# S5 products on VectorE alone, O in whole rows, layer 1's attention bias beside layer 0's merge

## The chip, the cores and the metric

One core of a Trainium2 chip runs the kernel, in float32, as one program. The metric is the device time of one execution in microseconds; several executions are taken and their median is given. TensorE's clock has two levels, 1.2 and 2.4 GHz; the profile shows what was granted, as a share of full speed.

## What is computed

A backbone of two layers over 512 latent tokens and 256 context tokens, 1024 channels. Each layer projects the normalised, modulated input by one wide matrix and hands the parts to three mixers: a bidirectional S5 state-space model, a neighbourhood attention with a learned bias by relative position, and a latent attention with compressed keys. Cut to what the change touches:

```python
h = layer_norm(x) * (1.0 + scale) + shift
(ua, za, qn, kn, vn, zn, cq, ckv, kr, zm, ga, gn, gm) = split_cols(h @ w_in)
# S5, for each direction d and each of 32 groups, state of 64 complex numbers:
s[t] = a * s[t - 1] + (bb @ u[t]);  y[t] = real(c @ s[t])
# neighbourhood attention: bias[h] = rpb[h, row offset, column offset], masked outside the window
s_lat = (q @ k.T) * NA_SCALE + bias
m = sig(ga) * ((ya * silu(za)) @ w_branch_a) + sig(gn) * ((yn * silu(zn)) @ w_branch_b) \
  + sig(gm) * ((ym * silu(zm)) @ w_branch_c)
x = layer_norm(DEEPNORM_ALPHA * x + gate * (m @ w_out))
```

The S5 recurrence is computed in chunks of 8 tokens. For that, small matrices are built from the parameters alone: W (inputs of a chunk to its state), O (state to outputs), the rotations R and the kernel K inside a chunk, out of powers of `a` and of B and C.

## The kernel before

A layer runs in five stages, each in a block `with phase(...)`: `s5a` (projections for S5, the gates and the compressed keys, and the S5 matrices), `na` (S5 itself and neighbourhood attention), `mla`, `mrg` (the merge, with gates and branch products) and `out`. A planner inside the compiler puts each engine's instructions and DMA issues in order from a timeline that it estimates; it draws on the order in the program. Every engine works off its list in that order, and so does SyncE's DMA queue, called `Q`, on which all DMAs of the parts that follow are issued.

Every matrix product is done in three float32r parts. A weight is loaded into one of four buffers `wr` (`wraw`, line 212), copied by ScalarE to `wh`, and the rest `wl` is a subtraction on VectorE or GpSimd (`split`, line 204), two buffers each; `gemm` (line 226) then runs the matmuls of line 233. The compressed keys have matmuls of their own at line 1054, with loads at line 1046.

`s5_build` (line 560) makes the S5 matrices of one block of 8 groups; there are four blocks a layer. `prm` holds tables of powers that `s5_tables` made. For each direction 12 elementwise products and sums run on `sb` tiles, a ring of six (`SB`, four in the merge): six for R (lines 630 to 636), three for O (649 to 651), three for W (677 to 679). Each string of `BE` says, letter by letter, which engine makes which of these 12: P is GpSimd, V is VectorE. `BE[0]` serves layer 0's four builds in its stage `s5a`, `BE[2]` layer 1's builds in layer 1's stage, `BE[1]` the builds of layer 1 that run early, in layer 0's merge, in halves of four groups. Results go to DRAM: R at line 637, O at 653, W at 684, K at 685, and from K the Toeplitz matrix by line 688. Line 661 holds the small matmuls on O that make K; line 679's result is transposed on TensorE. `s5_block` (line 692) loads these matrices in stage `na`, O at line 710, and multiplies with them.

`na_bias` (line 341) makes the attention bias of both layers: it writes the reversed, padded table to DRAM (`rpb_d`, line 348), then, for each layer and each pair of heads, three loads with overlapping rows fill a tile of the `sb` ring (line 359), GpSimd adds the mask `na_mk`, and line 361 stores it to `na_zd`. It is called once, in layer 0's stage `s5a`, by the letter N of `JOBS[0]`, the job order `uuBaBmaBmBacmaNmc`; B is a build, a and m are gate projections, c a half of the compressed keys, u an S5 input.

In layer 0's merge `SIDE[0]` says which side work goes before which of 24 steps: T makes layer 1's tables, B a build (`next_build`, line 1457), G gelu (line 1460) of S5's output, which closes the pools of T and B and takes memory behind them. Steps 0 to 7 are branch b, 8 to 15 branch c with its gates, from 16 on the remaining gates of branch a; then come the GLU products on gelu's result `ah`.

Of the kernel before, what the change touches and what calls it, by code (L numbers as in the profile page):

```python
# [78 lines left out]
BE = ('PPVVPVVPVVPV', 'VVPVVVVVVVVV', 'VPVVPVVPVVPV')  # L79
# [6 lines left out]
SIDE = ('T....B.B......G.........', '................G.......')  # L86
# [34 lines left out]
def build(tc, a, out):  # L121
# [219 lines left out]
    def na_bias(p, wk):  # L341
# [9 lines left out]
        zs = []  # L351
        for l in range(DEPTH):
            zd = T(dr, [48, 8, 480], f"na_zd{l}")
            for h2 in range(4):
                z = T(wk, [128, 1152], "sb", SB[0])[0:48, 0:960].rearrange("p (r c) -> p r c", c=32)
                for ty in range(3):
                    src = bass.AP(tensor=pd.tensor, offset=pd.offset + (l * 8 + 2 * h2) * 960 + 8 * ty,
                                  ap=[[1, 16], [64, 30], [1, 32]])
                    Q.dma_start(out=z[16 * ty:16 * ty + 16], in_=src)
                tt(P, z, z, mk.unsqueeze(1).to_broadcast([48, 30, 32]), ALU.add)  # L360
                Q.dma_start(out=zd[:, 2 * h2:2 * h2 + 2], in_=z.rearrange("p (h r) c -> p h (r c)", h=2))
            zs.append(zd)
        return zs
# [196 lines left out]
    def s5_build(l, b, prm, wk, ng, be, nsb, ni):  # L560
# [15 lines left out]
        od = [T(dr, [128, 1024], f"s5_o{l}{b}{d}") for d in range(2)]  # L576
# [38 lines left out]
        E = [V if c == 'V' else P for c in be]  # L615
        np_ = ng // 2
        for d in range(2):
            w = T(wk, [128, 1024], "s5_w", 1)
            for h in range(8 // ng):
# [10 lines left out]
                tt(E[0], rv[0], A[0], B[0], ALU.mult)  # L630
                tt(E[1], r1.rearrange("p c (x y) -> p c x y", x=6), A[1], B[1], ALU.mult)
                tt(E[2], rc[:, 0], rc[:, 0], r1, ALU.subtract)
                tt(E[3], rv[1], A[0], B[1], ALU.mult)
                r2 = sb(np_, 96)
                tt(E[4], r2.rearrange("p c (x y) -> p c x y", x=6), A[1], B[0], ALU.mult)
                tt(E[5], rc[:, 1], rc[:, 1], r2, ALU.add)
                Q.dma_start(out=rd[d][:, :, 96 * np_ * h:96 * np_ * (h + 1)], in_=rc.rearrange("p z c n -> p z (c n)"))
# [11 lines left out]
                tt(E[6], o, cc[0], pw[0], ALU.mult)  # L649
                tt(E[7], t, cc[1], pw[1], ALU.mult)  # L650
                tt(E[8], o, o, t, ALU.add)
# [25 lines left out]
                tt(E[9], x, bc[0], pw[0], ALU.mult)  # L677
                tt(E[10], t, bc[1], pw[1], ALU.mult)
                tt(E[11], x, x, t, ALU.add)
# [4 lines left out]
            Q.dma_start(out=wd[d], in_=w)  # L684
        Q.dma_start(out=kd.rearrange("x q n -> q x n"), in_=kds.rearrange("p x m i -> p x (m i)"))
# [6 lines left out]
    def s5_block(mats, b, m8, ud, yd, p, need_ctx):  # L692
# [10 lines left out]
        for d in range(2):  # L703
# [54 lines left out]
        for g in range(8):  # L758
            o = py[:, 512 * (g // 4) + 96 * (g % 4):][:, 0:NY]
            PE.matmul(o, tp[:, g], u[:, g, 32:32 + NY], start=True, stop=False)  # L760
            PE.matmul(o, ot[0][:, g], sd[0][:, g, 32:32 + NY], start=False, stop=False)
            PE.matmul(o, ot[1][:, g], sd[1][:, g, 1:1 + NY], start=False, stop=True)
# [903 lines left out]
```

## Time and profile before

| What | Value |
|---|---|
| Time, median of 3 runs | 1876.83 us (1871.46 to 1877.72) |
| The profiled execution | 1875.92 us, of which the span of the trace is 1874.1 us |
| TensorE matmul, busy | 1699.5 us, 91% |
| VectorE, busy | 1274.9 us, 68% |
| ScalarE, busy | 746.8 us, 40% |
| GpSimd, busy | 733.9 us, 39% |
| Mean granted clock of TensorE | 0.960 |
| DMA | 262.90 MB, mean 140 GB/s |

The table is an average over the whole span; what a change in one stage can be worth is read from that stage. In the rows, PE is TensorE, DVE VectorE, ACT ScalarE, POOL GpSimd and SP (SPq) SyncE with its DMA queue; L661 is line 661. A group's line names operation, output tile and input tiles, shapes and count.

### The profile page before, as it was taken

How to read it: one execution, taken by the hardware profiler on the slowest of the kernel's cores; microseconds unless marked ns; L12 is line 12 of the kernel's file. 1: busy time of each engine (PE TensorE's matmuls, PEld its weight loads, DVE VectorE, ACT ScalarE, POOL GpSimd, SP SyncE). 2: the span in 40 equal slices, each digit the busy share in tenths (PEclk: the TensorE clock that was granted, in tenths of full speed). 3: DMA queues.
4: the chain of work that ended last, by engine and by line, in shares of the span. 5: the costliest groups of instructions: out<-in, count | busy, mean ns of one | idle time of the engine just before them, and what ended most of it. 6: DMA issues, size and time to landing. Idle time of an engine off the chain costs nothing. (4 is left out here: it accounts for less than half of the span.)

```text
span 1874.1 us, 29013 instructions
## 1 busy us (share of the span) xinstructions
PE 1699.5 (91%) x10808; PEld 1406.4 (75%) x10808; DVE 1274.9 (68%) x2531; ACT 746.8 (40%) x1466; POOL 733.9 (39%) x472
## 2 busy tenths in 40 slices
PE   4877689999999999898999988799999999999987
PEld 2666578888878887777787766687888878788865
DVE  4999935687766556699735597944888866653267
ACT  4422233443365556222233335342444455652241
POOL 2177753223422111323445857723333221135373
PEclk9888899999999999999999999899999899999998
DMA  9546595443431120655637725565454332243362
GB/s 294 151 132 195 173 213 173 129 125 97 136 105 49 57 85 18 231 149 151 200 127 227 214 97 143 167 180 175 147 153 133 104 87 64 84 147 101 120 209 69
DMA packets 286388, 262.90 MB, mean 140 GB/s; under 512 B 70120, under 2 KB 243576, under 8 KB 286248
## 3 DMA queue, kind: packets, MB, share of 16 engines
q1 hardware_dynamic: 285048, 257.96, 46.8%
q0 software_dynamic: 1200, 3.10, 0.5%
q8 instruction: 85, 1.39, 0.3%
q14 instruction: 55, 0.45, 0.1%
HBM read 197.71 MB, written 67.48 MB: 142 GB/s over the span
## 5 line engine op out<-in xcount | busy, mean ns | idle before, releaser
L233 PE MATMUL g<-hh,wh 128*128 128x512 f32 (+1 forms) x1344 | 487.4, 364 | 15.8 <-DVE ua L900 7.4
L233 PE MATMUL g<-hh,wl 128*128 128x512 f32 (+1 forms) x1344 | 483.9, 361 | 8.1 <-POOL wl L146 5.7
L233 PE MATMUL g<-hl,wh 128*128 128x512 f32 (+1 forms) x1344 | 485.6, 362 | 3.9 <-DVE hl L149 2.2
L146 POOL TENSOR_TENSOR wl<-wr,wh 128x1024 fp32r<-128x1024 f32 (+2 forms) x94 | 231.5, 2464 | 481.6 <-ACT wh L143 465.6
L233 PEld LDWEIGHTS g<-hh,wh 128*128 128x128 f32 x1344 | 257.9, 192 | 61.7 <-issue 10.4
L233 PEld LDWEIGHTS g<-hh,wl 128*128 128x128 f32 x1344 | 258.2, 192 | 47.8 <-POOL wl L146 6.8
L233 PEld LDWEIGHTS g<-hl,wh 128*128 128x128 f32 x1344 | 258.2, 192 | 45.2 <-DVE hl L149 2.7
L143 ACT ACTIVATE wh<-wr 128x1024 fp32r<-128x1024 f32 (+1 forms) x150 | 155.2, 1035 | 261.4 <-PE g L233 154.9
L146 DVE TENSOR_TENSOR wl<-wr,wh 128x1024 fp32r<-128x1024 f32 (+1 forms) x56 | 86.8, 1550 | 88.8 <-ACT wh L143 87.3
L233 PE MATMUL g<-ah,wh 128*128 128x512 f32 (+1 forms) x336 | 120.3, 362 | 4.9 <-DVE macc L149 4.9
L233 PE MATMUL g<-al,wh 128*128 128x512 f32 (+1 forms) x336 | 120.4, 359 | 1.8 <-DVE al L146 1.8
L233 PE MATMUL g<-ah,wl 128*128 128x512 f32 (+1 forms) x336 | 118.5, 358 | 2.1 <-POOL wl L146 2.1
L143 ACT ACTIVATE mla_pt<-s 128x384 f32<-128x384 f32 (+1 forms) x128 | 59.4, 475 | 87.8 <-PE s L198 87.3
L1380 DVE TENSOR_REDUCE mla_sm<-w 128x1 f32<-128x768 f32 (+1 forms) x80 | 67.9, 849 | 34.4 <-PE w L1378 33.2
L146 DVE TENSOR_TENSOR sb<-sb 128x384 f32<-128x384 f32 (+4 forms) x72 | 86.6, 1214 | 0.2
L143 ACT ACTIVATE na_p<-w,na_sm 128x512 f32<-128x512 f32 (+1 forms) x80 | 50.9, 644 | 85.2 <-DVE na_sm L153 83.7
L233 PEld LDWEIGHTS g<-ah,wh 128*128 128x128 f32 x336 | 63.6, 190 | 19.7 <-DVE macc L149 5.8
L233 PEld LDWEIGHTS g<-ah,wl 128*128 128x128 f32 x336 | 63.8, 190 | 12.9 <-POOL wl L146 3.0
L233 PEld LDWEIGHTS g<-al,wh 128*128 128x128 f32 x336 | 63.9, 190 | 12.8 <-DVE al L146 2.5
L146 POOL TENSOR_TENSOR macc<-macc,g_t 128x768 f32<-128x768 f32 (+1 forms) x32 | 56.5, 1769 | 33.4 <-DVE g_t L149 33.4
L143 ACT ACTIVATE mla_p<-w,mla_sm 128x768 f32<-128x768 f32 (+1 forms) x80 | 65.0, 813 | 6.2 <-DVE mla_sm L153 6.0
L149 DVE SCALAR_TENSOR_TENSOR g_t<-g_t,g 128x512 f32<-128x512 f32 (+1 forms) x48 | 27.7, 592 | 57.5 <-PE g L233 56.4
(356 smaller groups left out, 3742.6 us busy)
## 6 DMA issues: line engine op xcount, KB each, us to landing
wr<-in_w_in SPq DMA_DIRECT2D x104, 512.0 KB, 4.4
wr<-in_w_mod SPq DMA_DIRECT2D x32, 512.0 KB, 4.6
s_w<-s_w SPq DMA_DIRECT2D x32, 512.0 KB, 4.3
s_o<-s_o SPq DMA_DIRECT2D x16, 512.0 KB, 4.3
wr<-in_w_out SPq DMA_DIRECT2D x16, 512.0 KB, 3.4
wr<-in_w_in SPq DMA_DIRECT2D x16, 416.0 KB, 4.6
s_o<-sb SPq DMA_DIRECT2D x12, 512.0 KB, 3.9
s_rc<-s_r SPq DMA_DIRECT2D x16, 384.0 KB, 3.3
```

What stands on the lines that cost most here:

```text
L143: return S.activation(out=o, in_=i, func=f, **kw)
L146: return e.tensor_tensor(out=o, in0=x, in1=y, op=op)
L149: V.scalar_tensor_tensor(out=o, in0=x, scalar=s, in1=y, op0=op0, op1=op1)
L233: PE.matmul(o, w[:, k], x[:, k, 0:n], start=(k == 0 and i == 0), stop=(k == nk - 1 and i == 2))
L1380: V.tensor_reduce(out=sm[:, 3:4], in_=q[:, k0:TOK], axis=AX.X, op=ALU.max)
```

## The change

All strings `BE` go: every product and sum of a build runs on VectorE, in layer 0's stage, in layer 1's stage and in the merge. O is written to DRAM as made, nine powers wide (1152 columns) and in one run per partition; `s5_block` loads 1136 columns of it and takes its matrices out of the row at a stride of 144. The bias is split into the table (`na_bias_rows`) and a function per layer: layer 0's still comes at N of `JOBS[0]`, layer 1's comes in layer 0's merge at the new letter N of `SIDE`, before step 10, in the merge's four `sb` buffers, one head at a time: 8 tiles with three loads, one GpSimd addition and one store each, where layer 0 has 4 tiles of two heads. `s5_build` has a parameter for the queue of its stores; its default is SyncE's queue and no call gives another. Besides, the table `m8` of layer 1 is allocated when it is made, an unused tile goes, and a small tile of the attention has 3 columns in place of 5.

```diff
-BE = ('PPVVPVVPVVPV', 'VVPVVVVVVVVV', 'VPVVPVVPVVPV')
-SIDE = ('T....B.B......G.........', '................G.......')
+SIDE = ('T....B.B..N...G.........', '................G.......')
...
-    def na_bias(p, wk):
+    def na_bias_rows(p):
...
         Q.dma_start(out=pd, in_=pad)
+        return pd
+
+    def na_bias_layer(l, pd, p, tag, bufs, size):
+
         mk = T(p, [48, 32], "na_mk")
         Q.dma_start(out=mk, in_=a["k_namask"])
...
+        zd = T(dr, [48, 8, 480], f"na_zd{l}")
+        nh = size // 480
+        for h in range(0, 8, nh):
+            z = T(p, [128, size + size // 5], tag, bufs)[0:48, 0:480 * nh].rearrange("p (r c) -> p r c", c=32)
+            for ty in range(3):
+                src = bass.AP(tensor=pd.tensor, offset=pd.offset + (l * 8 + h) * 960 + 8 * ty,
+                              ap=[[1, 16], [64, 15 * nh], [1, 32]])
+                Q.dma_start(out=z[16 * ty:16 * ty + 16], in_=src)
+            tt(P, z, z, mk.unsqueeze(1).to_broadcast([48, 15 * nh, 32]), ALU.add)
+            Q.dma_start(out=zd[:, h:h + nh], in_=z.rearrange("p (h r) c -> p h (r c)", h=nh))
+        return zd
...
-    def s5_build(l, b, prm, wk, ng, be, nsb, ni):
+    def s5_build(l, b, prm, wk, ng, nsb, ni, out_q=Q):
...
-        od = [T(dr, [128, 1024], f"s5_o{l}{b}{d}") for d in range(2)]
+        od = [T(dr, [128, 1152], f"s5_o{l}{b}{d}") for d in range(2)]
...
-        E = [V if c == 'V' else P for c in be]
...
-                tt(E[0], rv[0], A[0], B[0], ALU.mult)
-                tt(E[1], r1.rearrange("p c (x y) -> p c x y", x=6), A[1], B[1], ALU.mult)
+                tt(V, rv[0], A[0], B[0], ALU.mult)
+                tt(V, r1.rearrange("p c (x y) -> p c x y", x=6), A[1], B[1], ALU.mult)
...
-                s0 = 1 if d == 0 else 0
-                Q.dma_start(out=od[d].rearrange("p (g x) -> p g x", g=8)[:, g0:g0 + ng],
-                                    in_=o[:, :, s0:s0 + 8].rearrange("p g m i -> p g (m i)"))
+                out_q.dma_start(out=od[d][:, 144 * g0:144 * (g0 + ng)], in_=o.rearrange("p g m i -> p (g m i)"))
...
-            o = T(p, [128, 8, 128], "s5_o", 2)
-            Q.dma_start(out=o.rearrange("p g n -> p (g n)"), in_=od[d])
-            ot.append(o)
+            o = T(p, [128, 1136], "s5_o", 2)
+            Q.dma_start(out=o, in_=od[d][:, 16:1152] if d == 0 else od[d][:, 0:1136])
+            ot.append([o[:, 144 * g:144 * g + 128] for g in range(8)])
...
-                    zds.extend(na_bias(sp, sa))
+                    pds.append(na_bias_rows(sp))
+                    zds.append(na_bias_layer(0, pds[0], sa, "sb", SB[0], 960))
...
+                def next_bias():
+                    zds.append(na_bias_layer(l + 1, pds[0], side["b"], "sb", SB[1], 480))
...
-                    elif j in "TB" and need_ctx:
-                        {"T": next_tables, "B": next_build}[j]()
+                    elif j in "TBN" and need_ctx:
+                        {"T": next_tables, "B": next_build, "N": next_bias}[j]()
```

## Rows read from the trace of the kernel before

**Rows 1.** Busy us by engine from 86 to 226: PE, PEld, DVE, ACT, POOL, clock, DMA.

```profile
86.00:226.00 140.00, 101.49 (x586) 83.48 (x585) 137.36 (x170) 34.74 (x73) 98.89 (x45) 0.82 0.55 163
```

**Rows 2.** TensorE's waits, 86 to 226: who for whom, us, times, longest.

```profile
PE s L661 <- DVE sb L146: 20.7, 6, 5.7
```

**Rows 3.** Groups of VectorE by shape, 100 to 226: busy us, mean ns, idle before.

```profile
L146 DVE TENSOR_TENSOR sb<-s_b,s_p 128x1024 f32<-128x1024 f32 x8 | 23.2, 2895 | 0.0
L146 DVE TENSOR_TENSOR sb<-sb 128x384 f32<-128x384 f32 x16 | 19.0, 1196 | 0.0
L146 DVE TENSOR_TENSOR sb<-s_c,s_p 128x1152 f32<-128x1152 f32 x8 | 18.7, 2340 | 0.8 <-ACT s_c L143 0.7
L146 DVE TENSOR_TENSOR sb<-sb 128x1024 f32<-128x1024 f32 x7 | 12.4, 1775 | 0.0
L146 DVE TENSOR_TENSOR sb<-sb 128x1152 f32<-128x1152 f32 x7 | 12.1, 1723 | 0.0
L146 DVE TENSOR_TENSOR sb<-s_ta,s_tb 128x384 f32<-128x384 f32 x8 | 11.3, 1411 | 0.0
L146 DVE TENSOR_TENSOR wl<-wr,wh 128x1024 fp32r<-128x1024 f32 x3 | 9.5, 3163 | 0.0
L149 DVE SCALAR_TENSOR_TENSOR s_kds<-eye,s_dcol,s_kds 128x16 f32<-128x16 f32 x6 | 4.5, 789 | 0.0
```

**Rows 4.** Timeline of VectorE in layer 1's stage: start us, us, instruction.

```profile
1186.96 1.64 DVE L146 TENSOR_TENSOR sb<-s_ta,s_tb 128x384 f32<-128x384 f32 x2
...
1197.35 1.34 DVE L146 TENSOR_TENSOR sb<-s_c,s_p 128x1152 f32<-128x1152 f32 x1
1198.62 0.54 DVE L146 TENSOR_TENSOR sb<-sb 128x384 f32<-128x384 f32 x1
...
1200.42 1.21 DVE L146 TENSOR_TENSOR sb<-s_b,s_p 128x1024 f32<-128x1024 f32 x1
```

**Rows 5.** Groups of GpSimd by shape, 100 to 226.

```profile
L146 POOL TENSOR_TENSOR sb<-s_ta,s_tb 128x384 f32<-128x384 f32 x24 | 38.5, 1621 | 21.1 <-DVE sb L146 12.6 <-DVE s_tb L146 5.7 <-DMA s_r<-sb 2.9
L146 POOL TENSOR_TENSOR sb<-s_c,s_p 128x1152 f32<-128x1152 f32 x8 | 22.3, 2788 | 9.8 <-ACT s_c L143 6.6 <-DVE sb L146 2.2 <-DVE s_b L146 0.9
L146 POOL TENSOR_TENSOR sb<-s_b,s_p 128x1024 f32<-128x1024 f32 x8 | 21.7, 2714 | 6.6 <-DVE sb L146 6.6
L146 POOL TENSOR_TENSOR wl<-wr,wh 128x1024 fp32r<-128x1024 f32 x2 | 6.7, 3353 | 0.0
L146 POOL TENSOR_TENSOR wl<-wr,wh 128x832 fp32r<-128x832 f32 x2 | 5.2, 2586 | 0.0
```

**Rows 6.** Timeline of GpSimd: a short instruction of each shape, with the idle time before.

```profile
158.00 2.04 POOL L146 TENSOR_TENSOR sb<-s_b,s_p 128x1024 f32<-128x1024 f32 x1 [0.49 <-DVE sb L146]
...
184.21 2.25 POOL L146 TENSOR_TENSOR sb<-s_c,s_p 128x1152 f32<-128x1152 f32 x1 [0.50 <-DVE sb L146]
...
1173.31 1.09 POOL L146 TENSOR_TENSOR sb<-s_ta,s_tb 128x384 f32<-128x384 f32 x1 [1.29 <-DVE sb L146]
```

**Rows 7.** Timeline of SyncE's queue and of TensorE behind the bias loads.

```profile
255.88 3.94 SPq L359 DMA_DIRECT2D sb<-rpb_d  x7
259.86 0.99 SPq L1046 DMA_DIRECT2D wr<-in_w_in  x2
...
266.27 0.71 PE L1054 MATMUL w<-wh,hh 128*128 128x416 f32 x1 [3.39 <-ACT wh L143]
```

**Rows 8.** TensorE's waits in layer 1's build stage, 1140 to 1226.

```profile
PE s L661 <- DVE sb L146: 6.7, 1, 6.7
```

**Rows 9.** Timeline of GpSimd: one bias addition of two heads.

```profile
232.17 2.24 POOL L146 TENSOR_TENSOR sb<-sb,na_mk 48x960 f32<-48x960 f32 x1
```

**Rows 10.** Timelines of layer 0's merge: gelu's first loads, last `ah`, first matmul on it.

```profile
919.46 1.01 SPq L1469 DMA_DIRECT2D y<-y_d  x2
...
954.41 0.85 ACT L143 ACTIVATE ah<-gf 128x768 fp32r<-128x768 f32 x1 [0.69 <-DVE gf L149]
...
984.54 0.50 PE L233 MATMUL g<-ah,wh 128*128 128x512 f32 x1
```

More of the change, by code (lines that the diff above doesn't have):

```diff
@@ L629, in s5_build @@
                 rv = [rc[:, z].rearrange("p c (x y) -> p c x y", x=6) for z in range(2)]
-                tt(E[0], rv[0], A[0], B[0], ALU.mult)
-                tt(E[1], r1.rearrange("p c (x y) -> p c x y", x=6), A[1], B[1], ALU.mult)
-                tt(E[2], rc[:, 0], rc[:, 0], r1, ALU.subtract)
-                tt(E[3], rv[1], A[0], B[1], ALU.mult)
+                tt(V, rv[0], A[0], B[0], ALU.mult)
+                tt(V, r1.rearrange("p c (x y) -> p c x y", x=6), A[1], B[1], ALU.mult)
+                tt(V, rc[:, 0], rc[:, 0], r1, ALU.subtract)
+                tt(V, rv[1], A[0], B[1], ALU.mult)
                 r2 = sb(np_, 96)
-                tt(E[4], r2.rearrange("p c (x y) -> p c x y", x=6), A[1], B[0], ALU.mult)
-                tt(E[5], rc[:, 1], rc[:, 1], r2, ALU.add)
-                Q.dma_start(out=rd[d][:, :, 96 * np_ * h:96 * np_ * (h + 1)], in_=rc.rearrange("p z c n -> p z (c n)"))
+                tt(V, r2.rearrange("p c (x y) -> p c x y", x=6), A[1], B[0], ALU.mult)
+                tt(V, rc[:, 1], rc[:, 1], r2, ALU.add)
+                out_q.dma_start(out=rd[d][:, :, 96 * np_ * h:96 * np_ * (h + 1)], in_=rc.rearrange("p z c n -> p z (c n)"))
                 def powers(n, rev):
@@ L676, in s5_build @@
                 bc = [z[:, d, g0:g0 + ng].unsqueeze(2).to_broadcast([128, ng, 8, 16]) for z in (b1t, b2t)]
[L677 to L679 removed]
+                tt(V, x, bc[0], pw[0], ALU.mult)
+                tt(V, t, bc[1], pw[1], ALU.mult)
+                tt(V, x, x, t, ALU.add)
                 q = ps_groups()
@@ L683, in s5_build @@
                 act(w[:, 128 * g0:128 * (g0 + ng)], q[:, 0:128 * ng])
-            Q.dma_start(out=wd[d], in_=w)
-        Q.dma_start(out=kd.rearrange("x q n -> q x n"), in_=kds.rearrange("p x m i -> p x (m i)"))
+            out_q.dma_start(out=wd[d], in_=w)
+        out_q.dma_start(out=kd.rearrange("x q n -> q x n"), in_=kds.rearrange("p x m i -> p x (m i)"))
         for j in range(8):
@@ L760, in s5_block @@
             PE.matmul(o, tp[:, g], u[:, g, 32:32 + NY], start=True, stop=False)
-            PE.matmul(o, ot[0][:, g], sd[0][:, g, 32:32 + NY], start=False, stop=False)
-            PE.matmul(o, ot[1][:, g], sd[1][:, g, 1:1 + NY], start=False, stop=True)
+            PE.matmul(o, ot[0][g], sd[0][:, g, 32:32 + NY], start=False, stop=False)
+            PE.matmul(o, ot[1][g], sd[1][:, g, 1:1 + NY], start=False, stop=True)
         for s in range(2):
@@ L833, in build @@
         mods = [T(base, [128, 3, 8, 2], f"mod{l}") for l in range(DEPTH)]
-        m8s = [T(base, [128, 32], f"s5_m8{l}") for l in range(DEPTH)]
+        m8s = [T(base, [128, 32], "s5_m8")]
         mats = [[], []]
@@ L837, in build @@
         dcols = T(base, [128, DEPTH, 4, 2], "s5_dcol")
-        zds = []
-        ones = T(base, [128, 1], "ones")
-        V.memset(ones, 1.0)
+        zds, pds = [], []
         for l in range(DEPTH):
@@ L1178, in na_scores @@
                                               stop=(j == 1))
-                        sm = T(nap, [128, 5, 2], "na_sm", 3)
+                        sm = T(nap, [128, 3, 2], "na_sm", 3)
                         pr = T(nap, [128, 2, 512], "na_p", 2)
@@ L1447, in next_tables @@
                     side["p"] = sides.enter_context(tc.tile_pool(name="s5p", bufs=1, reuse_waits="tile"))
+                    m8s.append(T(base, [128, 32], "s5_m8"))
                     with tc.tile_pool(name="s5t", bufs=1, reuse_waits="tile") as wk:
```

31 lines of the change are left out of this document (9 added, 22 removed).

## The prediction

> **What bounds the kernel now.** I read the profile in three steps. First the busy times by stretch. TensorE is the engine whose end is the kernel's end, so what counts is where it is not busy. The widest such place is layer 0's S5 stage: from 86 to 226 us TensorE is busy 101.49 of 140 us while VectorE is busy 137.36 and GpSimd 98.89 [rows 1]. VectorE is full there, TensorE is not, and its granted clock is 0.82 of full speed on average, a mix of its two levels. Second, TensorE's waits in that stretch: the largest is for VectorE's `sb` tiles ahead of the small matmuls of line 661, 20.7 us in 6 waits [rows 2]. So this stage ends when VectorE has worked through its queue, and a microsecond taken off that queue is a microsecond off the kernel, as long as TensorE keeps idle time to give. Third, what VectorE does in it, shape by shape [rows 3], against the same shapes at a place where GpSimd is not reading SBUF [rows 4], and what GpSimd does [rows 5].
>
> The reader is to see this: a 128x1024 product takes VectorE 1.21 us when alone and 2895 ns on average here, a 128x1152 one 1.34 against 2340 ns, a 128x384 sum 0.54 against 1196 ns. VectorE is full, but nearly half of its time it stands inside an instruction that GpSimd holds up. The change moves GpSimd's products to this full engine, so the whole question is whether the time lost to GpSimd is larger than the work taken over.
>
> **Layer 0's builds (lines 630 to 679).** Of 12 products and sums per direction five run on GpSimd. In the stretch 100 to 226 us those are 24 of 128x384, 8 of 128x1152 and 8 of 128x1024 [rows 5]; all 40 go to VectorE.
>
> Time given back: the measured sums of the eight rows [rows 3] less count times the lone duration [rows 4]. Products 128x1024: 23.2 - 8 x 1.21 = 13.5. Sums 128x384: 19.0 - 16 x 0.54 = 10.4. Products 128x1152: 18.7 - 8 x 1.34 = 8.0. Sums 128x1024: 12.4 - 7 x 1.21 = 3.9. Sums 128x1152: 12.1 - 7 x 1.34 = 2.7. Products 128x384, lone 1.64 / 2 = 0.82: 11.3 - 8 x 0.82 = 4.7. That is 43.2 us. The weight splits (9.5 for three) and the six tiny `s_kds` instructions (4.5) are held up as well; with 1.21 as the lone time of a 128x1024 split and, as an estimate, 0.2 for the 16-column instruction, 5.9 and 3.3 more: 52.4 us. GpSimd keeps its weight splits, 6.7 + 5.2 of its 94.4 us [rows 5], 12.6%, and I leave that share of the loss in place: 45.8 us come back.
>
> Time added: 24 x 0.82 + 8 x 1.34 + 8 x 1.21 = 40.1 us. But neighbours overlap a little: the 1.34 us sum that starts at 1197.35 is followed by a start at 1198.62, 1.27 later [rows 4], so each of the 40 costs 0.07 less in a full queue: 37.3 us. Net 45.8 - 37.3 = 8.5, I take **8 us off**. Lower end: only the loss inside the build's own instructions is given back, 0.874 x 43.2 = 37.8 against 40.1, 2 us slower. Upper end: the lone GpSimd durations are all given back, 24 x 1.09 + 8 x 2.25 + 8 x 2.04 = 60.5 [rows 6], against 37.3: 23 us faster. I stay near the lower end because VectorE's own rows measure the loss, and GpSimd's durations only what could be lost.
>
> The Trainium skill bears on this (SBUF — State Buffer, "Who interferes with whom"): a VectorE instruction with two SBUF inputs and a GpSimd instruction that reads SBUF exclude each other for the whole instruction. By it the sum would stand near the upper end, since all that GpSimd reads for would be given back. The rows agree that one holds up the other, but show less than that time lost.
>
> What is late next: VectorE again, with the same `z` and `wl` instructions in its queue; TensorE's 38.5 us of idle time [rows 1] is far more than 8, so the gain is not cut off there. A product written into the ring of six `sb` buffers also waits until the store of an older tile in that buffer has landed; with a faster VectorE that cover shrinks. Its price, where it bites, is inside the bounds above.
>
> **Layer 0's attention bias (lines 350 to 364).** Twelve loads, four stores and four GpSimd additions of layer 1 leave this stage. Their cost is visible: the queue issues seven bias loads from 255.88 on, 3.94 us, and only then, at 259.86, the next two weight loads of line 1046; TensorE then waits 3.39 us at 266.27 for the ScalarE copy of that weight [rows 7]. With half the bias gone the last burst is gone and these loads are issued up to 3.94 us earlier. I take **4 us off** (the 3.39 and a little for the slower matmuls after the pause); ends 0, if the planner puts something else ahead of the weights, and 8, twice that, if the other bursts held back weights too.
>
> **Layer 1's own builds** (two in the stage, four GpSimd instructions of 12, so 16 in all): at layer 0's rate 16 / 40 x 8.5 = 3.4. TensorE's largest wait for `sb` there is 6.7 us [rows 8], the most this line can give. I take **3 us off**, ends 0 and 7.
>
> **Layer 0's merge.** Eight 128x192 subtractions change from GpSimd to VectorE: at most the 0.54 us of twice that size, 4.3 us on VectorE, against two handovers saved each time. I take 0, ends -2 and +4. New is layer 1's bias at step 10: 24 loads, 8 stores, 8 GpSimd additions of half size. At 0.56 us an issue (3.94 / 7, [rows 7]) the queue has 18 us more to issue (32 x 0.56). It sits in SyncE's queue ahead of the gates' weight loads and of the `y` loads of gelu; on GpSimd the additions, an estimated 1.1 us each, half of the 2.24 of a full one [rows 9], stand ahead of weight splits, `macc` sums and the `y_t` products, and each waits for its three loads. Who waits for that: TensorE for weights, as at 266.27. One such stall is 3.39 us; I take **4 us more**, ends 0 (four weight buffers hide it) and 10 (three stalls). Gelu can't take its memory until the bias stores have landed. Now its first loads go out at 919.46, its last `ah` is made at 954.41 + 0.85, and the first matmul on it starts at 984.54 [rows 10]: 29.3 us of cover for 18 us of issue and two rounds through four buffers. I cost that at nothing; without the cover every microsecond beyond 29.3 is one of TensorE's.
>
> **O as whole rows.** The store becomes one run per partition instead of eight pieces, the load of the S5 stage carries 1136 instead of 1024 columns. Neither stands in a wait of TensorE's that I use; 0, and at worst a fraction of a microsecond for each of the eight S5 blocks. All else (`na_sm` columns, `m8s`, `ones`) is 0: same instructions, other addresses. `out_q` has SyncE's queue as its default and no caller changes it, so no copy changes its queue.
>
> **Sum.** The profiled execution took 1875.92 us, span 1874.1; the median of three is 1876.83, 0.9 more, so I work from the former. 1875.9 - 8 - 4 - 3 + 4 = 1864.9: **1865 us**, 0.6% faster.
>
> **Rivals.**
> (a) The planner orders TensorE's work by a timeline of its own. With one engine in place of two that hold each other up, its order may fit the chip better, so that TensorE runs projections where it now stands before line 661. For it: 20.7 us in six waits [rows 2]. Against: VectorE's sum above still has to be done before the stage is over, unless projections of later jobs fill the time. Price: these waits gone instead of the 8: 1865 - 13 = 1852, and down to 1844 with the upper ends of the bias and layer 1.
> (b) A wash: what layer 0 and 1 gain, about 11, is given back in the merge (10) or in waits for the `sb` ring. For it: the bias did hold up TensorE where it stands now [rows 7]. Against: 29.3 us of cover for gelu and four weight buffers. Time: about 1875.
> (c) Slower: VectorE is the bound and gets 37 us of work. If GpSimd's presence costs it less than the rows suggest, because VectorE's rows here are long for waits inside the instruction that have another cause, say half of 52.4, then 26 come back, 11 are added in layer 0 and 4 in layer 1, and with the bias (-4 + 4) the time is 1891. It decides from the point at which less than 37.3 of the 52.4 comes back. For it: VectorE has 2.6 us idle in 140 [rows 1]. Against: the same shapes a thousand microseconds later, on the same engine, take under half [rows 3, 4].
> That the change doesn't do what it says is no rival: engine and place are fixed in the code; only the planner's order is open.
>
> **How the numbers follow.** Forecast (1853 to 1871) 0.48, (a) 0.16, (b) 0.22, (c) and a late gelu together 0.14. About 0.3% is what a measurement of this kernel can tell from no change, that is 1871.2 to 1882.5. Faster: 0.48 + 0.16 = 0.64; within: 0.22; slower: 0.14. The range reaches to (a)'s lower end and over all of (b): 1844 to 1882, leaving out about 0.18.
>
> **What would show it.** Right: in the build stage the 128x1152 and 128x1024 instructions of VectorE take 1.2 to 1.4 us, GpSimd does only weight splits, and the last `sb` transposes of layer 0, now before 220 us, come some 8 us earlier; no 3.4 us stop in the second line-1054 group; in the merge 8 bias additions, with gelu's end still ahead of the first matmul on it. Wrong: VectorE's instructions stay long, or TensorE's waits for `sb` grow; waits of VectorE for `s_r` or `s_o` stores; TensorE waiting for weights or for `ah` between 905 and 990 us.

## The result, and the profile after

| | before | after |
|---|---|---|
| median of the runs, us | 1876.99 (4 runs, 1871.46 to 1877.72) | 1852.05 (4 runs, 1848.12 to 1853.13) |
| profiled execution, us | 1875.92 | 1853.01 |
| its span, us | 1874.1 | 1851.1 |

The ratio is 0.9861, with an interval of 0.9845 to 0.9876 (on a second chip 0.9829, 0.9812 to 0.9846): 24.9 us or 1.3% faster, where 11.8 were forecast. The time lies inside the range (1844 to 1882), and beside rival (a)'s 1852. So the direction held, and the question is where the other 13 us come from.

The build stage after, to be set against [rows 1] and [rows 2]. First the busy times by stretch: its length, then PE, PEld, DVE, ACT and POOL with their counts of instructions, the granted clock, DMA share and GB/s.

```profile
86.00:226.00 140.00, 114.28 (x742) 98.00 (x744) 137.57 (x228) 44.73 (x98) 27.30 (x9) 0.90 0.61 191
```

And TensorE's waits in it (us in total, times, longest):

```profile
PE s L659 <- DVE sb L145: 12.8, 4, 8.0
PE g L232 <- DVE wl L145: 4.4, 1, 4.4
PE g L1051 <- POOL wl L145: 3.8, 1, 3.8
```

VectorE is as full as before (137.57 against 137.36 us), but GpSimd is down from 98.89 to 27.30, and TensorE has run 742 matmuls in the stretch in place of 586. Its longest sum of waits is still for `sb`, 12.8 us in place of 20.7 (line 659 is line 661 of before).

The instructions of VectorE by shape, from 95 to 226 us, and GpSimd's; these answer [rows 3] and [rows 5]:

```profile
L145 DVE TENSOR_TENSOR sb<-s_ta,s_tb 128x384 f32<-128x384 f32 x32 | 29.8, 962 | 0.0
L145 DVE TENSOR_TENSOR sb<-s_c,s_p 128x1152 f32<-128x1152 f32 x16 | 23.2, 1469 | 0.0
L145 DVE TENSOR_TENSOR sb<-s_b,s_p 128x1024 f32<-128x1024 f32 x16 | 20.9, 1334 | 0.0
L145 DVE TENSOR_TENSOR sb<-sb 128x1024 f32<-128x1024 f32 x8 | 11.2, 1399 | 0.0
L145 DVE TENSOR_TENSOR sb<-sb 128x1152 f32<-128x1152 f32 x8 | 10.8, 1352 | 0.0
L145 DVE TENSOR_TENSOR sb<-sb 128x384 f32<-128x384 f32 x16 | 10.6, 674 | 0.0
L148 DVE SCALAR_TENSOR_TENSOR s_kds<-eye,s_dcol,s_kds 128x16 f32<-128x16 f32 x6 | 1.2, 238 | 0.0
...
L145 POOL TENSOR_TENSOR wl<-wr,wh 128x1024 fp32r<-128x1024 f32 x4 | 15.3, 3824 | 49.2 <-ACT wh L142 49.2
```

VectorE now does 96 build instructions in 106.5 us; before it did 54 in 96.7, and GpSimd 40 more in 82.5 beside it. The 128x1024 product went from 2895 to 1334 ns. GpSimd's weight splits did not get shorter: 3824 ns, against 3353 in [rows 5] and 2.33 us for the one that starts at 42 us, ahead of the builds.

**The whole run by stages.** The stages of both layers overlap at their ends, so I cut the trace at instructions that every kernel has: the first `na_q` activation of a layer, its first `mla_q` activation, the first matmul on `ah` of layer 0's merge, and the last `hh<-macc` of a layer. The lengths between them, in us of each kernel's one profiled execution ("again" is a second profiled execution of the changed kernel, on another chip):

| stretch | before | after | again | engines_alone | bias_alone | bias_back |
|---|---|---|---|---|---|---|
| start to layer 0's `na_q` | 283.2 | 257.9 | 258.1 | 266.5 | 275.4 | 268.4 |
| `na` of layer 0 | 273.8 | 273.4 | 275.4 | 281.4 | 274.1 | 283.4 |
| `mla` of layer 0 | 211.6 | 210.8 | 210.3 | 212.2 | 211.8 | 210.9 |
| merge of layer 0 | 279.1 | 289.1 | 289.2 | 276.7 | 288.2 | 277.7 |
| to layer 1's `na_q` | 230.5 | 230.7 | 230.3 | 227.9 | 231.2 | 227.0 |
| `na` of layer 1 | 228.9 | 225.5 | 229.2 | 229.8 | 229.5 | 224.7 |
| to layer 1's last `hh<-macc` | 312.3 | 309.8 | 310.8 | 312.8 | 313.1 | 309.7 |

All of the gain is made before layer 0's first `na_q` (25.3 us); the merge gives 10.0 back, and layer 1 adds some 6 in the one execution and 1 to 2 in the other. Differences of 2 to 4 us in one stage can't be told from the scatter between executions.

### The profile page after: what moved, and what is told of

Same layout as the page of the kernel before. It is cut to its first block, busy times and chain, and to the rows that moved or that the text cites. A ratio compares the mean times of both kernels' runs of the same rounds, so it can differ in the third digit from the quotient of the medians.

```text
span 1851.1 us, 29023 instructions
## 1 busy us (share of the span) xinstructions
PE 1684.5 (91%) x10808; PEld 1407.5 (76%) x10808; DVE 1253.8 (68%) x2594; ACT 746.0 (40%) x1466; POOL 627.7 (34%) x412
## 5 line engine op out<-in xcount | busy, mean ns | idle before, releaser
L145 POOL TENSOR_TENSOR wl<-wr,wh 128x1024 fp32r<-128x1024 f32 (+2 forms) x94 | 246.2, 2621 | 583.6 <-ACT wh L142 573.8
L145 DVE TENSOR_TENSOR wl<-wr,wh 128x1024 fp32r<-128x1024 f32 (+1 forms) x56 | 76.2, 1361 | 92.6 <-ACT wh L142 92.4
L232 PEld LDWEIGHTS g<-ah,wh 128*128 128x128 f32 x336 | 63.6, 190 | 16.7 <-issue 3.9
L145 DVE TENSOR_TENSOR sb<-sb 128x384 f32<-128x384 f32 (+3 forms) x80 | 69.4, 880 | 0.3
L145 DVE TENSOR_TENSOR sb<-s_ta,s_tb 128x384 f32<-128x384 f32 (+1 forms) x80 | 68.8, 896 | 0.3
```

Of the source, the lines that this page charges most:

```text
L145: return e.tensor_tensor(out=o, in0=x, in1=y, op=op)
L232: PE.matmul(o, w[:, k], x[:, k, 0:n], start=(k == 0 and i == 0), stop=(k == nk - 1 and i == 2))
```

## The experiments

**1. The parts of the change one by one.**

engines_alone: the kernel before with every product and sum of the builds on VectorE.

```diff
-BE = ('PPVVPVVPVVPV', 'VVPVVVVVVVVV', 'VPVVPVVPVVPV')
+BE = ('VVVVVVVVVVVV', 'VVVVVVVVVVVV', 'VVVVVVVVVVVV')
```

> Only the engines of the S5 products change (all on VectorE, in all three places); O, the bias and small tiles stay as before. If the engines make the gain of layer 0's S5 stage (in the changed kernel neighbourhood attention's first query tile starts 25.3 us earlier), this kernel's first query tile starts 17 to 25 us earlier than before's 283.2 us, the merge (first branch matmul to last copy of macc) keeps its 279 us, and the whole gains 20 to 33 us. If the bias made a good part of it, as I had it with 4 us of 12, no more than 17 to 20 us are left; if the bias's burst was the main thing, under 12.

Measured: 1864.63 us, ratio 0.9936 (0.9916 to 0.9956). That is 12 to 14 us off, below the 20 to 33 expected if the engines made all of the gain; the first `na_q` comes 16.7 us earlier (17 to 25 expected).

bias_alone: the kernel before with only layer 1's bias moved to the merge.

```diff
-SIDE = ('T....B.B......G.........', ...
+SIDE = ('T....B.B..N...G.........', ...
-                    zds.extend(na_bias(sp, sa))
+                    zds.append(na_bias_layer(0, pds[0], sa, "sb", SB[0], 960))
```

> Only the bias moves: layer 0's in the stage, layer 1's before step 10 of layer 0's merge, all else as before. By my sum 4 us off in layer 0's S5 stage and 4 us on in the merge: no difference. By the traces of before and after, in which the merge is 10 us longer: 3 to 8 off and 10 on, so 2 to 7 us slower than before. If the bias carried the gain of the stage, 10 us faster or more.

Measured: 1879.03 us, ratio 0.9996 (0.9977 to 1.0016): no difference, as by the prediction's sum, and not the 2 to 7 us slower read from the two traces.

rows_alone: the kernel before with O stored as whole rows, `na_sm` smaller, layer 1's `m8s` made late and no `ones`.

```diff
-        od = [T(dr, [128, 1024], f"s5_o{l}{b}{d}") for d in range(2)]
+        od = [T(dr, [128, 1152], f"s5_o{l}{b}{d}") for d in range(2)]
-        ones = T(base, [128, 1], "ones")
```

> Only O's whole rows, with the smaller tiles that make room for them; engines and bias as before. Both my theory and its rivals give no difference beyond 3 us; a gain of 5 us or more would mean that the eight pieces per partition held up the ring of sb tiles.

Measured: 1874.2 us, ratio 0.9987 (0.9969 to 1.0005), no difference, as expected.

bias_back: the changed kernel with both layers' bias in layer 0's stage.

```diff
-SIDE = ('T....B.B..N...G.........', ...
+SIDE = ('T....B.B......G.........', ...
-                    zds.append(na_bias_layer(0, pds[0], sa, "sb", SB[0], 960))
+                    zds.extend(na_bias_layer(l_, pds[0], sa, "sb", SB[0], 960) for l_ in range(DEPTH))
```

> The changed kernel with both layers' bias made in layer 0's S5 stage again. If the move costs what the merge's 10 us say and brings 3 to 8 in the stage, this kernel is 2 to 7 us faster than the changed one, at 1845 to 1850 us, with a merge of 279 us in place of 289; if the move is a wash, the same as the changed one.

Measured: 1855.6 us, ratio 0.9887 (0.9851 to 0.9924), slower than the 1845 to 1850 expected if the move costs more than it brings.

What follows. The engines are about half of the gain, and the bias and the rows alone are nothing that can be told from zero; together the parts give more than their sum (the three ratios multiply to 0.992, against 0.986). Which of them add to each other, the whole times don't say: bias_back has the engines and the rows without the bias move, and its interval reaches over that of the changed kernel. To see it in the stages, I cut the build stage once more, at the last transpose of a layer 0 `sb` tile on TensorE: up to it the builds run, and behind it stands what is left of the projections. Here are the two stretches of the kernel before, columns as above:

```profile
86.00:232.80 146.80, 108.29 (x633) 88.98 (x632) 144.09 (x177) 37.96 (x85) 104.64 (x49) 0.83 0.55 163
232.80:283.20 50.40, 43.59 (x231) 38.31 (x230) 19.49 (x37) 16.73 (x36) 25.43 (x16) 0.93 0.95 219
```

The same two of engines_alone:

```profile
86.00:225.10 139.10, 117.62 (x754) 99.37 (x754) 137.94 (x232) 45.24 (x99) 24.69 (x9) 0.92 0.63 191
225.10:266.50 41.40, 30.80 (x144) 26.71 (x142) 18.98 (x22) 14.00 (x32) 25.36 (x13) 0.87 0.83 168
```

The tail of bias_alone:

```profile
233.80:275.40 41.60, 40.63 (x231) 36.58 (x229) 17.29 (x30) 16.73 (x36) 13.59 (x11) 1.00 0.87 233
```

And both stretches of the changed kernel:

```profile
86.00:228.60 142.60, 116.88 (x756) 100.14 (x755) 139.42 (x233) 45.09 (x99) 27.53 (x10) 0.90 0.60 189
228.60:257.90 29.30, 24.54 (x112) 22.27 (x111) 7.62 (x16) 9.90 (x22) 15.08 (x11) 0.86 0.79 201
```

The engines bring the end of the builds from 232.8 to 225.1, 7.7 us earlier, which is the 8 us of the forecast. But the tail behind it is shorter too, 41.4 us in place of 50.4, since only 144 matmuls are left in it in place of 231: TensorE has run 754 during the builds, in place of 633. TensorE takes its instructions in a fixed order, and this order is another one: ahead of the seventh of the first eight groups of small matmuls (line 661), 489 projection matmuls stand in the program of before, and 648 in that of engines_alone and of the changed kernel. The bias leaves the builds' end where it was (233.8) and takes its 8.8 us from the tail: the same 231 matmuls, with 1.0 us of idle time in place of 6.8, and at full clock in place of 0.93.

With both edits the tail is down to 112 matmuls and 29.3 us. So of the 25.3 us that come back before layer 0's `na_q`, 4.2 are an earlier end of the builds (228.6 against 232.8) and 21.1 a shorter tail. And without the bias move, the faster stage runs into its own bias. The first 40 us of layer 0's `na` in the changed kernel:

```profile
257.90:297.90 40.00, 38.91 (x276) 33.86 (x275) 21.81 (x39) 14.36 (x27) 15.76 (x13) 1.00 0.68 206
```

And in bias_back:

```profile
268.40:308.40 40.00, 33.48 (x205) 29.01 (x206) 23.07 (x31) 8.57 (x16) 12.30 (x15) 0.81 0.66 194
```

205 matmuls in place of 276, 6.5 us of idle time, and a granted clock of 0.81, a mix of the two levels. On SyncE's queue of bias_back the bias is right ahead of this (start us, us, instruction):

```profile
249.92 2.79 SPq L361 DMA_DIRECT2D sb<-rpb_d  x5
252.75 2.71 SPq L215 DMA_DIRECT2D wr<-in_w_in  x3
255.55 1.72 SPq L363 DMA_DIRECT2D na_zd<-sb  x1
257.36 0.38 SPq L215 DMA_DIRECT2D wr<-in_w_in  x1
257.84 4.38 SPq L363 DMA_DIRECT2D na_zd<-sb  x3
```

So `na` takes 283.4 us there and 281.4 in engines_alone, against 273 to 275 in the changed kernel, before, bias_alone and rows_alone, that is with one layer's bias or with the slower builds (268.2 to 276.9 in all the other kernels with faster builds and one layer's bias). That is a part of the gain that neither edit has alone: against the changed kernel's 273.4 the bias move is worth 8 to 10 us in `na`, but only once the builds are faster. It isn't all of it: in bias_back layer 1's `na` is 5 and its last stage 3 us shorter than in engines_alone, with the bias in the same place.

TensorE's two long stops in these 40 us of bias_back are for VectorE's `na_q` (2.9 us) and `na_kl` (3.4). S5's loads of `s_u` go out at 267.47 us, behind the bias stores, and in the changed kernel at 250.66, 7 us ahead of the stage. That the stores and loads in the queue are what holds up the start of `na` is read from these rows, not tried by itself. The same trace has a second way for the bias to cost time, GpSimd's last additions and VectorE's small `rms_v` instructions beside them:

```profile
257.45 4.43 POOL L145 TENSOR_TENSOR sb<-sb,na_mk 48x960 f32<-48x960 f32 x2
257.63 2.11 DVE L145 TENSOR_TENSOR rms_v<-rms_v 128x6 f32<-128x6 f32 x1
263.14 2.18 ACT L142 ACTIVATE ct<-ct,rms_v 128x256 f32<-128x256 f32 x6 [8.80 <-DVE rms_v L148]
```

In the changed kernel no addition stands beside it:

```profile
255.78 0.17 DVE L145 TENSOR_TENSOR rms_v<-rms_v 128x6 f32<-128x6 f32 x1
```

The instruction takes 2.11 us in place of 0.17, ScalarE waits 8.8 us for the `rms_v` that scales `ct`, and TensorE waits 4.7 us for `ct` in the tail. No run parts this from the queue.

**2. Is it GpSimd's reading?** The changed kernel, with GpSimd work added beside layer 0's builds that nobody needs.

pool_reads: 56 products of the identity with itself.

```diff
+        def beside(n_):
+            if dum is not None:
+                idn = ident.unsqueeze(1).to_broadcast([128, 3, 128])
+                for _ in range(n_):
+                    tt(P, dum, idn, idn, ALU.mult)
...
+                beside(1)
                 tt(V, rv[0], A[0], B[0], ALU.mult)
```

> The changed kernel with nothing moved back: 56 products of 128x384 of the identity with itself, into a scratch tile that nobody reads, are added on GpSimd beside layer 0's builds, as much GpSimd time as the kernel before had there in products and sums (56 x 1.09 us alone = 61). TensorE's instructions stand in the order of the changed kernel. Theory of contention (GpSimd's reads of SBUF hold VectorE up, so that VectorE's full queue ends later): VectorE's 128x1024 and 128x1152 instructions go from 1.3-1.5 us back towards 2 to 3 us, layer 0's first na_q, at 257.9 us in the changed kernel, comes 20 to 45 us later, and the whole takes 1872 to 1897 us. Rival (the gain came from the other order in which the planner sets TensorE's work, or from handovers between the engines that are gone): nothing waits for these products and the order is kept, so 1848 to 1857 us, and VectorE's durations as they are.

Measured: 1875.46 us, ratio 0.9981 (0.9957 to 1.0005). The first `na_q` came at 282.1 us, 24.2 later, with TensorE's order unchanged. Two points of the expectation failed, though: the products waited for nothing, so GpSimd ran all of them ahead, from 14 to 110 us and beside the tables, and VectorE's build instructions stayed short. It was the tables that grew long: their 26 `s_v` instructions of 128x96 with two input tiles took 596 ns on average in place of 340, and the first `sb<-s_bb` of the builds starts at 112.1 us in place of 88.6. The last `sb` transpose started at 250.1, and the tail was 32.0 us, as in the changed kernel. So a shorter tail goes with the order, and the builds' end with VectorE.

pool_writes: the same places, with `P.memset(dum, 0.0)` for the product.

> The same 56 places as in pool_reads, but a memset of 128x384 instead of the product: GpSimd is as often occupied, and only writes SBUF. If it is GpSimd's reading that holds VectorE up: VectorE's durations stay at 1.3-1.5 us for 128x1024 and 128x1152, the first na_q stays within 3 us of 257.9, the whole within 1846 to 1859 us. If any GpSimd instruction on SBUF does it: as pool_reads in proportion to the memsets' time, at 0.3 to 1 us each 17 to 56 us of GpSimd, so 1860 us or more.

Measured: 1847.65 us, ratio 0.9825 (0.9793 to 0.9856). Nothing is lost in the whole time; the first `na_q` comes at 263.0 us, 5.1 later than in the changed kernel where at most 3 were expected, and `na` is 5.2 us shorter. The memsets, too, ran ahead of the builds, from 14 to 53 us.

tied_reads and tied_writes put the same work where it was meant to be: GpSimd first copies one column of the VectorE product that has just been written.

```diff
+                P.tensor_copy(out=dum[:, 0, 0:1], in_=t_)
+                for _ in range(n_):
+                    tt(P, dum, idn, idn, ALU.mult)
...
                 tt(V, rv[0], A[0], B[0], ALU.mult)
+                beside(rc[:, 0, 0, 0:1], 1)
```

> The changed kernel with the 56 GpSimd products of pool_reads, now tied to their places: after each of VectorE's five products per direction that GpSimd had before, GpSimd copies one column of it and then multiplies the identity with itself, 1, 1, 1, 2 and 2 times 128x384. So GpSimd reads while the builds run, and not ahead of them during the tables, where the products of pool_reads went. If GpSimd's reads are what made the builds' VectorE instructions long: between 95 and 226 us VectorE's 128x1152 and 128x1024 products go from 1469 and 1334 ns to over 1900 ns on average, 128x384 sums from 674 to over 900, the first na_q comes 12 to 35 us after 257.9, and the whole takes 1860 to 1885 us. Rival (reading holds up only what ran beside it in pool_reads, the tables' short instructions, or the long durations of before came from handovers): durations within 15% of the changed kernel's, the first na_q within 6 us, the whole 1845 to 1857 us.

> As tied_reads, with memsets of 128x384 for the products: the same waits of GpSimd for VectorE and the same column copies, but GpSimd only writes (0.42 us each in pool_writes, 24 us in all). If reading is the cause: VectorE's durations as in the changed kernel, first na_q 255 to 263 us, the whole 1844 to 1856 us. If it is GpSimd's waiting in its order (weight splits behind a wait for VectorE) that costs in tied_reads: the same loss as there.

Measured: tied_reads 1874.98 us, ratio 0.9992 (0.9977 to 1.0007); tied_writes 1850.82 us, ratio 0.987 (0.9843 to 0.9897). VectorE's groups from 95 to 226 us, and GpSimd's added one, of tied_reads:

```profile
L145 DVE TENSOR_TENSOR sb<-s_c,s_p 128x1152 f32<-128x1152 f32 x12 | 21.1, 1768 | 0.0
L145 DVE TENSOR_TENSOR sb<-s_b,s_p 128x1024 f32<-128x1024 f32 x12 | 15.6, 1323 | 0.0
L145 DVE TENSOR_TENSOR sb<-sb 128x1152 f32<-128x1152 f32 x6 | 12.7, 2116 | 0.0
L145 DVE TENSOR_TENSOR sb<-sb 128x384 f32<-128x384 f32 x14 | 11.3, 816 | 0.5 <-POOL dum L621 0.5
...
L145 POOL TENSOR_TENSOR dum<-ident 128x384 f32<-128x384 f32 x45 | 60.3, 1339 | 3.4
```

And of tied_writes:

```profile
L145 DVE TENSOR_TENSOR sb<-s_c,s_p 128x1152 f32<-128x1152 f32 x15 | 22.0, 1476 | 0.0
L145 DVE TENSOR_TENSOR sb<-sb 128x1152 f32<-128x1152 f32 x7 | 9.5, 1350 | 0.0
L145 DVE TENSOR_TENSOR sb<-sb 128x384 f32<-128x384 f32 x15 | 10.0, 678 | 0.0
...
L623 POOL MEMSET dum<- 128x384 f32 x52 | 21.7, 418 | 2.9
```

With reads the sums that follow a GpSimd product go from 1352 to 2116 ns (128x1152) and from 674 to 816 (128x384), the 128x1152 products from 1469 to 1768; the 128x1024 products stay (1323 against 1334), for a reason that no run here gives. With writes all stay. The builds end at 255.0 us with reads, at 234.8 with writes, at 228.6 in the changed kernel; the tails are 30.8, 29.7 and 29.3. So GpSimd's reads beside the builds cost 20 us more than its writes at the same places, and these 20 us are inside VectorE's instructions: its 112 on `sb` tiles ahead of `na_q` are busy 125.7 us with reads and 105.6 with writes. That the whole time with reads is that of before is chance: before had 40 products fewer on VectorE and another order on TensorE. The whole times held for both kernels, and the first `na_q` (285.8 us with reads; 264.5 with writes, 1.5 above what was expected); over 1900 ns for the products and over 900 for the 128x384 sums was too high.

**3. What the bias costs in the merge.** The timelines of SyncE's queue, ScalarE and TensorE in layer 0's merge of the changed kernel; line 215 is the load of a weight:

```profile
895.90 3.83 SPq L361 DMA_DIRECT2D sb<-rpb_d  x8
900.26 0.31 SPq L363 DMA_DIRECT2D na_zd<-sb  x1
900.62 0.94 SPq L361 DMA_DIRECT2D sb<-rpb_d  x2
901.73 0.32 SPq L363 DMA_DIRECT2D na_zd<-sb  x1
902.09 2.42 SPq L361 DMA_DIRECT2D sb<-rpb_d  x5
904.65 0.34 SPq L363 DMA_DIRECT2D na_zd<-sb  x1
905.10 0.40 SPq L215 DMA_DIRECT2D wr<-in_w_in  x1
...
909.41 1.06 ACT L142 ACTIVATE wh<-wr 128x1024 fp32r<-128x1024 f32 x1 [6.27 <-DMA wr<-in_w_in]
...
910.51 0.80 PE L232 MATMUL g<-hh,wh 128*128 128x512 f32 x1 [6.89 <-ACT wh L142]
```

The weight load goes out at 905.10, behind the bias; ScalarE copies it 4.3 us later, and by then TensorE has stood for 6.89 us. Its clock is 0.90 from 900 to 950 us, where it was 1.00 from 900 to 950 before. Against bias_back the merge is 11.4 us longer: 7.5 of these are idle time of TensorE, 3.9 longer busy time of the same 1560 matmuls. Four kernels tried to take this away from the changed kernel.

bias_spread: one head at each of eight merge steps.

```diff
-SIDE = ('T....B.B..N...G.........', ...
+SIDE = ('TNNNNBNBNNN...G.........', ...
```

> The changed kernel with layer 1's attention bias cut into its eight heads, one head at each of eight steps of the merge (steps 1 to 4, 6, 8, 9 and 10), 3 loads, 1 store and 1 addition a step, in place of all eight heads at step 10. Theory of the queue (32 issues in a row on SyncE's queue hold back the gates' weight loads behind them, and TensorE stops for these): the merge, 288.8 us from layer 0's first ah to its last hh, goes back to about 279 us, the gap of 6.9 us for ScalarE's wh near 910 us is gone, and the whole takes 1840 to 1846 us. Rival (what the bias costs in the merge is the issues and additions themselves, wherever they stand, or the later memory of gelu): 1849 to 1856 us, the merge still 286 to 290.

Measured: 1850.49 us, ratio 0.9838 (0.9804 to 0.9872); merge 284.5 us. The spreading reached the queue in part: the additions of five heads are done by 858 us, but the loads of the last three still go out from 895.77 on, eight of them in a row, and TensorE's stop for `wh` is 5.5 us in place of 6.9. The merge lies between the two expectations, the whole time in the rival's range. So it tells little.

bias_actq: the 32 issues on ScalarE's queue.

```diff
-                    zds.append(na_bias_layer(l + 1, pds[0], side["b"], "sb", SB[1], 480))
+                    zds.append(na_bias_layer(l + 1, pds[0], side["b"], "sb", SB[1], 480, S))
```

> The changed kernel with layer 1's 24 bias loads and 8 stores at step 10 of the merge issued by ScalarE in place of SyncE; nothing else moves. Theory of SyncE's queue: the weight loads behind the bias go out at once, the merge takes 279 to 283 us in place of 288.8, the whole 1842 to 1847 us. Rival (the issues cost whichever engine makes them, since ScalarE copies the weights that TensorE waits for, and a store that waits for its addition stops ScalarE): 32 x 0.5 = 16 us of ScalarE ahead of the copies to wh, merge 289 to 300, whole 1852 to 1864 us.

Measured: 1862.6 us, ratio 0.9913 (0.9885 to 0.9942); merge 298.4 us. The rival was right, as ScalarE's queue, ScalarE and TensorE show:

```profile
906.16 6.24 ACTq L361 DMA_DIRECT2D sb<-rpb_d  x6
912.44 0.38 ACT L142 ACTIVATE g_t<-g 128x256 f32<-128x256 f32 x1 [19.36 <-DMA sb<-rpb_d]
912.72 1.05 ACT L142 ACTIVATE wh<-wr 128x1024 fp32r<-128x1024 f32 x1
...
913.82 0.80 PE L232 MATMUL g<-ah,wh 128*128 128x512 f32 x1 [15.53 <-ACT wh L142]
```

ScalarE's own copies now stand behind its issues, and TensorE waits 15.53 us at one place.

bias_l1_mid (the first new line) and bias_l1_late (the second): layer 1's bias in layer 1's own S5 stage.

```diff
-JOBS = ('uuBaBmaBmBacmaNmc', 'maaBmmaBcamucuuu')
+JOBS = ('uuBaBmaBmBacmaNmc', 'maaBmmaBcaNmucuuu')
+JOBS = ('uuBaBmaBmBacmaNmc', 'maaBmmaBcamucNuuu')
```

> The changed kernel with layer 1's attention bias taken out of the merge and made in layer 1's own S5 stage, behind its second build (12 loads, 4 stores, 4 additions, as layer 0's is made). If the place in the merge is what costs 10 us there: merge 276 to 280 us in place of 288.8, layer 1's stage (last hh to first na_q, 230.7 us) 3 to 8 us longer, as the bias of one layer cost in layer 0's stage, and the whole 1845 to 1850 us. Rival (one layer's bias costs about the same 8 to 10 us wherever it is issued): stage 238 to 242 us, whole 1850 to 1855 us. In bias_back the stage of layer 1 without this bias took 227.0 us after a merge without it, so the sum of both stages would be at best 277 + 227 = 504 against 519.5 of the changed kernel.

> As bias_l1_mid, but the bias stands ahead of the last three jobs of layer 1's stage, where VectorE is busy only 17 of 40 us and 2 of 22 us, and no build follows it. If what the bias costs is its place in SyncE's queue ahead of builds' copies and weight loads: less than in bias_l1_mid, stage 227 to 232 us, whole 1838 to 1846 us. Rival (the loads of weights at the end of the stage are what TensorE waits for, and the issues stand ahead of them, or the attention's first tile waits for the stored bias): stage 235 to 242 us, whole 1847 to 1855 us.

Measured: 1846.73 us, ratio 0.9831 (0.981 to 0.9852), and 1844.74 us, ratio 0.9825 (0.9798 to 0.9851). The merge is 275.2 and 273.6 us without the bias, 14 to 16 less; but layer 1's stage goes from 230.7 to 237.3 and 236.7. bias_l1_late missed its 227 to 232: late in the stage it costs as much as in the middle. To see whether the rest is a gain, the changed kernel and bias_l1_late ran on one chip.

> The changed kernel as it is, beside bias_l1_late2 on one chip. All theories: 1849 to 1854 us.

> The same kernel as bias_l1_late, to set it against the changed kernel on one chip. If the bias costs more in the merge than late in layer 1's stage: 1842 to 1848 us, 4 to 9 us under the changed kernel. If the earlier difference was that of two chips: within 3 us of it.

Measured: the changed kernel 1846.77 us (six runs, 1841.45 to 1859.07, below the 1849 to 1854 expected), ratio 0.9829 (0.9812 to 0.9846); bias_l1_late 1842.77 us (five runs, 1837.73 to 1850.32), ratio 0.9823 (0.98 to 0.9846). The two can't be told apart. One layer's bias makes each of the three stages in which it was tried 6 to 16 us longer, and no version beats the changed kernel by an amount that was shown.

**4. The last 2 to 3 us.** small_alone: rows_alone without the whole rows.

```diff
-                        sm = T(nap, [128, 5, 2], "na_sm", 3)
+                        sm = T(nap, [128, 3, 2], "na_sm", 3)
-        ones = T(base, [128, 1], "ones")
```

> The kernel before with the three small tiles of the change alone: na_sm of 3 columns, m8s of layer 1 made in the merge, no ones; O is stored as before. rows_alone held these and the whole rows. If the 128x512 matmuls on hh and hl are faster by where their tiles lie (394 ns in place of 398 in the last stage of rows_alone and of the changed kernel, 398 to 399 before and in engines_alone): 394 here too, the whole 1870 to 1876 us. If whole rows did it (less traffic beside them): 398 to 399, the whole as before.

Measured: 1875.58 us, ratio 0.9996 (0.9982 to 1.001). The matmuls on `hl` with `wh` in layer 1's last stage, of before:

```profile
L233 PE MATMUL g<-hl,wh 128*128 128x512 f32 x176 | 70.3, 399 | 0.0
```

Of engines_alone:

```profile
L233 PE MATMUL g<-hl,wh 128*128 128x512 f32 x172 | 68.7, 399 | 0.0
```

Of small_alone:

```profile
L233 PE MATMUL g<-hl,wh 128*128 128x512 f32 x176 | 69.3, 394 | 0.0
```

Of the changed kernel:

```profile
L232 PE MATMUL g<-hl,wh 128*128 128x512 f32 x176 | 69.3, 394 | 0.0
```

5 ns a matmul, or 1.0 us in these rows and 2.8 with the 352 matmuls on `hh` with `wh` and on `hh` with `wl`, come with the small tiles and not with the whole rows. Taking tiles out moves the ones behind them; that the place of `hh` and `hl` is the reason is argued, not shown. In the whole time it can't be seen.

## Why the prediction fell short, step by step

**Layer 0's builds, 8 us off: the sum was right, the step to the end of the stage was not.** VectorE's busy time from 86 us to the first `na_q` fell from 163.6 to 156.9 us in engines_alone, 6.7 us against the 8.5 worked out; with the 37.3 us that it took over, 44.0 came back, against 45.8. The builds end 7.7 us earlier. The step that failed is the sentence "this stage ends when VectorE has worked through its queue". The kernel before ends it 50.4 us after that, with 231 matmuls that TensorE had left; the prediction let this tail stand as it was, and engines_alone shortened it by 9.0 us as well. The stage gave 16.7, twice the step, still inside its bounds of 2 slower to 23 faster. With both edits it gave 25.3 where 12 were forecast, 4.2 at the end of the builds and 21.1 in the tail. Two readings behind the sum were loose without harm: the 0.2 us put for `s_kds` measured 238 ns, and one of the lone rows [rows 4], at 1200.42, has a GpSimd copy beside it from 1200.63 on.

**Rival (a) was half of the answer.** The order of TensorE's work did come out better, as the 231 and 144 matmuls of the tail show, and it did so by filling the idle time before line 661 with projections, the one condition the prediction named for it. But it was set beside the forecast as an alternative to the 8 us, where the two add up, builds and tail. What the order is worth by itself no run shows: pool_reads has the order of the changed kernel and a tail 18.4 us shorter than before, but its builds end 17.3 us later than before, with all products on VectorE and the time that GpSimd's reads cost it. That the measured time stands beside this rival's 1852 is luck: it priced the 20.7 us ahead of line 661 as gone, 12.8 of them are left, and the stage gave more than it said and the merge took back more.

**The layer 0 bias, 4 us off.** bias_alone gave 7.8, at the upper bound: TensorE's idle time in the tail fell by 5.8 us, more than the one stop of [rows 7], and the clock did the rest, 1.00 in place of 0.93. The price of the slower matmuls after a pause was put at "a little"; here it is 3.0 us. The further 8 to 10 us in `na` had no term at all. I asked what the bias holds back where it stands, not what it would hold back once the builds ahead of it are faster. One sign of being right failed in the changed kernel: TensorE still stops 3.45 us in the second group of line 1054, at 241.46, now for GpSimd's `wl`.

**Layer 1's builds, 3 us off.** 2.6 in engines_alone and 3.5 in bias_back; in the changed kernel 0.2 the other way. No gain is shown: rows_alone, with the old engines, takes 228.2 us for this stage and small_alone 230.9, and pool_reads and bias_actq, with the same bias in the merge as the changed kernel, take 227.4 and 227.5. The merge isn't the reason for the 0.2; what is stays open.

**The merge, 4 us more.** It was 10.0, the upper end, and 11.4 against bias_back. The mechanism was as told, bias issues ahead of weight loads, but one stop took 6.89 us in place of 3.39, and the slower matmuls behind it came on top, 3.9 us that had no term. The additions took 1.2 us each (estimate 1.1). Gelu did no harm, as forecast:

```profile
915.39 0.82 SPq L1470 DMA_DIRECT2D y<-y_d  x2
...
944.28 0.84 ACT L142 ACTIVATE ah<-gf 128x768 fp32r<-128x768 f32 x1 [0.66 <-DVE gf L148]
...
968.00 0.50 PE L232 MATMUL g<-ah,wh 128*128 128x512 f32 x1
```

The cover is 22.9 us in place of the 29.3 of [rows 10].

**Whole rows and small tiles, 0.** Nothing that the whole time shows; the 2.8 us of the last stage were not foreseen.

**Rival (c)** fell: VectorE took over all 40 products and was shorter busy. **Rival (b)** was right about the 10 us in the merge, but these came off 25 and not 11.

**Reads and writes.** The Trainium skill (SBUF — State Buffer, "Who interferes with whom") says that a VectorE instruction with two SBUF inputs contends with a GpSimd instruction that reads SBUF and not with one that only writes it. tied_reads and tied_writes agree: 2116 and 1350 ns for the 128x1152 sum. Its lock for a whole instruction would give back all of GpSimd's lone time, the upper end of 60.5 us; the 44.0 that came back, and tied_reads' 20 us beside its write-only twin for 56 products, are less. The prediction read the lock as if VectorE alone did the waiting; GpSimd's 40 products took 82.5 us against 60.5 alone [rows 5, rows 6], so a part of it was GpSimd's. Of the two ends the prediction was right to stay at the lower one for VectorE's sum.

The prediction also put the last `sb` transposes of before ahead of 220 us; they start until 232.8.

## What to carry to other kernels

A stage that waits for a full engine still ends with the engine that has work left over: look how much of its work stands behind the last wait, and ask whether the order will change along with the first engine. Two edits that touch one queue are to be costed together, since the stage that one of them shortens can move the transfers of the other onto the next stage (8 to 10 us here, read from the traces). And a queue that issues in order charges a burst of small transfers to whoever's load stands behind them, wherever the burst is put; here one layer's 16 to 32 issues cost 6 to 16 us in each of the places tried, and 9 us more on ScalarE's queue, where copies that TensorE needs stand behind them.

## What the runs showed of the hardware

- GpSimd is held up as well: its 128x384 product takes 940 ns on average beside the tables' short instructions (pool_reads, 95 to 226 us), and 1339 ns beside the builds (tied_reads); its weight split of 128x1024 takes 2.33 us at 42 us and 3824 ns beside the builds.
- GpSimd's copy of a single column took 848 ns on average in tied_reads and 1203 ns in tied_writes (95 to 226 us), where a memset of 128x8 takes 0.1 us. That it waits inside the instruction is read from this, not tried.
- A 128x512 float32r matmul on the same operands took 399 ns in layer 1's last stage of the three kernels with the old small tiles (before, engines_alone, bias_alone) and 394 in that of all others; in small_alone the small tiles are the only edit.
